# Context stream handled beside x in the first stage, own buffers for modulation blocks, and a later place for the last part of the filter network

## The chip, the core and the metric

The kernel runs on one core of a Trainium2 chip. The core has a matrix engine (PE, with its weight loads shown as PEld), a vector engine (DVE), an activation engine (ACT), a general engine (POOL, GpSimd) and a queue engine (SP) that issues most of the loads from memory. Each engine works through its own list of instructions in order and waits on semaphores for the others. The metric is device time in microseconds (us), the median of several runs; less is better.

## What is computed

Two layers of a diffusion backbone over 256 latent tokens with 2048 channels, with 256 context tokens beside them in the first layer. Cut to what matters here:

```python
sh1, sc1, g1, sh2, sc2, g2 = split(silu_c @ ada_w[l] + ada_b[l], 6)
h = rmsnorm(x, norm_g[l, 0]) * (1.0 + sc1) + sh1
# even layer (l = 0)
cmod = split(silu_cc @ ada_w[l][:, :2 * D_MODEL] + ada_b[l][:2 * D_MODEL], 2)
hc = rmsnorm(ctx, norm_g[l, 0]) * (1.0 + cmod[1]) + cmod[0]
y = hgrn_conv_mixer(h, hc, w_in, ...)       # first step: h @ w_in, and hc @ w_in[:, :3072]
x = x + g1 * y
x = x + g2 * (square(relu((rmsnorm(x) * (1 + sc2) + sh2) @ w1)) @ w2)
# odd layer (l = 1): Hyena. Its filters do not depend on x:
hdn = sin(freq * (z @ fw1 + fb1)); hdn = sin(freq * (hdn @ fw2 + fb2)); hdn = sin(freq * (hdn @ fw3 + fb3))
filt = hdn @ fw4
```

All products are made from fp32 values that are split into a high part and a low part, with three matmuls for each product (high by high, high by low, low by high).

## The kernel before

**The first stage** (`layer0` up to `pump_to(56)`) multiplies both streams, x and the context, with the first 3072 columns of the input weights ("w0"). The 2048 rows of the product (the channels) come in 16 tiles of 128, called kt. What a tile needs before its first matmul is its modulation: `ada_start(kt)` loads two blocks of 1 MB (shift and scale) and multiplies them on PE with both conditioning vectors (L212), ACT copies the result (L528), two small matmuls pick the rows (L531) and DVE adds the bias into `mod` (L533). `h_make` then makes the high and low parts of the normed tile, `hh` and `hl` for x, `uh` and `ul` for the context (L542 to L551). The norm's inverse root `rstd` of each stream is `norm_rstd` (L321 on PE, then L310 to L315).

The tiles are taken in four blocks of 1, 2, 5 and 8 (KBLOCKS). A block runs over column chunks: three of 1024 columns in block 0 and block 1, twelve of 256 in blocks 2 and 3. In each chunk the weights are loaded into a `raw` buffer (L660), ACT makes `whi` (L151), DVE makes `wlo` (L152), and PE multiplies the x side and then the context side (`block_mm`, L574 and L577). The results are added into `zz`, `v` for x and `czz`, `cv` for the context (L589 by ACT in block 0; L591, L595 by DVE later).

At the head of each chunk, `self.pump(1)` loads one further modulation block of 1 MB, which DVE multiplies by `sil` (L182; "PUMP" in the words below). While block b runs, `ada_start` is called for the tiles of block b + 1.

**Buffers.** All of these loads (w0 chunks, both blocks of `ada_start`, PUMP blocks) share the pool tag `raw`, with three buffers of 1 MB. A load is issued by SP, in SP's order, when the buffer's last reader is done.

**Order.** The statements inside `with self.in_order()` (block 0 and the preparation of tiles 0 to 2) keep the written order on each compute engine. Everywhere else a list scheduler, run when the program is built, fixes the order of each engine.

**The filter network.** `filter_net` runs on POOL from the start for more than 1300 us. Its last layer, `filter_tail`, transposes its result `h2` on PE (L1124, L1128), lets DVE scale it (`cv`, L1130), lets POOL take two sines of 29 instructions each (L1156 to L1181), and has DVE split the result into `h3h`, `h3l` (L1138, L1139). It stands in the loops of the first MLP, `mlp_body(0)`; the split is first used at the start of `hyena`. One step of those loops, `gemm_as`, makes 96 matmuls of 512 columns in eight half-megabyte pieces, each with one `whi` and one `wlo`.

Of the kernel before, what the change touches and what calls it, by code (L numbers as in the profile page):

```python
# [12 lines left out]
F32 = mybir.dt.float32  # L13
# [3 lines left out]
U8 = mybir.dt.uint8  # L17
# [4 lines left out]
P = 128  # L22
D = 2048
T = 256
KT = 16
# [38 lines left out]
class Kernel:  # L64
# [396 lines left out]
    def layer0(self):  # L461
# [3 lines left out]
        def s8(name, shape, dt=F32):  # L465
            t = pa.tile(shape, dt, tag="s8", name=name, bufs=3)
            return t

        silt = self.silt
        cct = pa.tile([P, 2, 2, KT], F32, tag="s2", name="cct", bufs=3)  # L470
        nc.sync.dma_start(out=cct[:, 0], in_=I["cct"])
# [9 lines left out]
        for lst, src in ((xq, "xT"), (cq, "ctxT")):  # L481
            for g in range(4):
                t = self.quad("x4", F32)
                nc.sync.dma_start(out=t[:, :, :T], in_=I[src][:, g * 4:g * 4 + 4, :])
                lst.append(t)
            if src == "xT":
                first = [self.ada_load(0, ch, 0, fa[:, ch, :]) for ch in range(2)]
                nc.sync.dma_start(out=self.sm, in_=I["sm"])
                chunks, _ = phase0_chunks()
                w0 = I["w0"]  # L490
                k0, nkt, row = chunks[0]
                assert nkt == 1
                loads = []
                for c0, cw, off in row:
                    r = fw[:, c0:c0 + cw]
                    nc.sync.dma_start(out=r, in_=bass.AP(w0.tensor, w0.offset + off, [[cw, P], [1, cw]]))
                    loads += [(c0, r[:, g * 256:g * 256 + 1024], list(range(g, g + 4)))
                              for g in range(0, cw // 256, 4)]
        ahead = {kt: [self.ada_load(0, ch, kt, s8("first", [P, D]) if kt == 2 and ch else None) for ch in range(2)]
                 for kt in kb[1]}  # L500
        xf = lambda kt: xq[kt // 4][:, kt % 4, :T]
        cf = lambda kt: cq[kt // 4][:, kt % 4, :T]
        nc.vector.memset(self.onesd, 1.0 / D)
        make_identity(nc, self.ident)
        masks = pa.tile([P, len(LEVELS), P], U8, name="masks")

# [15 lines left out]
        def ada_start(kt, raws=None):  # L522
            ps = self.psx()
            for ch in range(2):
                r = raws[ch] if raws else self.ada_load(0, ch, kt)
                self.ada_mm(ps[:, ch * P:(ch + 1) * P], r)
            sb = self.tmp(2 * P, "sq", 2)
            nc.scalar.activation(out=sb, in_=ps[:, :2 * P], func=AF.Copy)  # L528
            for ch in range(2):
                o = 2 * P + ch * 2  # L530
                nc.tensor.matmul(ps[:, o:o + 2], lhsT=sb[:, ch * P:(ch + 1) * P], rhs=self.selr, start=True,  # L531
                                 stop=True)
            self.last = nc.vector.tensor_tensor(  # L533
                out=view(self.mod, kt, [[192, 2], [16, 2]]), in0=view(ps, 2 * P, [[1, 2], [2, 2]]),
                in1=view(self.sm, SM["adab"][0] + kt, [[0, 2], [16, 2]]), op=ALU.add).ins
# [62 lines left out]
        with self.in_order():  # L598
# [10 lines left out]
            for i in range(4):  # L609
                square(xq, qx, i)  # L610
            for i in range(1, 4):
                qadd(nc.vector, qx, 0, i)
            rst.append(self.norm_rstd([qx[0][:, j, :T] for j in range(4)]))
            ada_start(0, first)
# [8 lines left out]
            for n, (c0, _, cgs) in enumerate(loads):  # L623
                block_mm(0, 0, 1, c0, *units[n], cgs, [0], 0, self.psx)
                if n < 2:
                    square(cq, qc, n * 2)
                    square(cq, qc, n * 2 + 1)
            ada_start(1, ahead[1])
            for i in range(1, 4):
                qadd(nc.vector, qc, 0, i)  # L630
            rst.append(self.norm_rstd([qc[0][:, j, :T] for j in range(4)]))
            h_make(0, 1, 1)
            for n, (c0, _, cgs) in enumerate(loads):
                block_mm(0, 0, 1, c0, *units[n], cgs, [0], 1)
            for side in range(2):
                h_make(1, 2, side)
            ada_start(2, ahead[2])
            for side in range(2):
                h_make(2, 3, side)
        self.filter_net(self.last)  # L640
# [4 lines left out]
        nc.vector.scalar_tensor_tensor(out=self.sil, in0=self.sil, scalar=1.0, in1=sr, op0=ALU.add, op1=ALU.mult)  # L645
        lbt = self.lb_setup()
        for b, (k0, nkt, row) in list(enumerate(chunks))[1:]:
# [35 lines left out]
        self.pump_to(56)  # L683
        self.ada_stop = 72
        self.new_u()
        self.dump("zz", zz)
# [25 lines left out]
        def s2(name):  # L712
            t = pa.tile([P, 512], F32, tag="s2", name=name, bufs=3)
            return t
# [33 lines left out]

        gh = pa.tile([P, NH], F32, name="gh")
        nc.vector.tensor_scalar(out=gh, in0=self.s_("gn", 0, 8), scalar1=0.5, scalar2=None, op0=ALU.mult)  # L750
        onehot = pa.tile([P, NH, NH], F32, name="onehot")
        nc.vector.memset(onehot, 0.0)
# [11 lines left out]
        def group(g0, par):  # L764
            qg = qq[g0 // 4][:, g0 % 4:g0 % 4 + G, :T]
            kq = s8("kq", [P, 4, W]) if par == 0 else st["kq1"]
            at = pa.tile([P, G, 2, T], F32, tag="s4", name="at", bufs=2)
            kd = s2("kd")
# [69 lines left out]
        def readout():  # L838
            rr = self.rsqrt(st["msq"][:NH, :T], NH, T)
            sel = pa.tile([NH, NH, P], F32, tag="s4", name="sel", bufs=2)  # L840
# [51 lines left out]
        for hh in range(2):  # L892
            nc.sync.dma_start(out=self.x[:, hh * 8:hh * 8 + 8, :], in_=I["xT"][:, hh * 8:hh * 8 + 8, :])
        self.pump_until(0, 2)

# [36 lines left out]

    def lb_setup(self):
        nc, cp = self.nc, self.cp
        self.zeros = self.pa.tile([P, T], F32, name="zeros")
        nc.vector.memset(self.zeros, 0.0)
        lg = self.s_("lb", 0, 48).rearrange("p (d l h) -> p d l h", d=2, l=3)
        mx = self.pa.tile([P, 2, NH], F32, name="lbm")
        e = self.pa.tile([P, 2, 3, NH], F32, name="lbe")
        s = cp.tile([P, 2, NH], F32, name="lbs")  # L940
# [37 lines left out]
    def mlp_body(self, l):  # L978
# [6 lines left out]
        for c in range(4):  # L985
# [10 lines left out]
            for g in range(4):  # L996
                if c == 3 and g == 2:
                    self.pump_to(self.ada_stop)
                if c == 2 and g == 0 and l == 0:
                    self.filter_tail()  # L1000
# [532 lines left out]
```

## Time and profile before

| what | us |
|---|---|
| median of 3 runs (2953.35 to 2958.92) | 2955.95 |
| the profiled execution | 2951.54 |
| its span, first to last instruction | 2949.7 |
| PE busy in it | 2788.0 (95%) |
| DVE busy | 2156.1 (73%) |
| POOL busy | 1560.0 (53%) |
| ACT busy | 1257.8 (43%) |

The profiled execution is one run, 4.4 us below the median; 1.8 us of it lie outside the span. An engine's busy time says little by itself: PE is the busiest, so what counts is the time in which PE stands, or runs at the lower of its two clocks (1.2 instead of 2.4 GHz). "PEclk" is the granted clock as a share of the higher one.

### The profile page before, as it was taken

The numbers are of one execution on the slowest core, as the hardware profiler recorded it, in microseconds if no ns is written. First come the engines' busy times: TensorE is split into PE (matmuls) and PEld (weight loads), VectorE is DVE, ScalarE is ACT, GpSimd is POOL, SyncE is SP. The second block draws the span as 40 slices with busy tenths as digits, with TensorE's granted clock in tenths as the row PEclk, the third lists the DMA queues.
The fourth block names the chain that finished last, engine by engine and source line by source line (L and its number), as shares of the span: only waits on it lengthen the run. The fifth ranks groups of instructions, "written<-read, shape, count | busy, mean of one in ns | idle before, by whom it ended". The sixth has DMA issues, their size and how long they took to land.

```text
span 2949.7 us, 46145 instructions
## 1 busy us (share of the span) xinstructions
PE 2788.0 (95%) x18508; PEld 2456.1 (83%) x18508; DVE 2156.1 (73%) x2599; ACT 1257.8 (43%) x1674; POOL 1560.0 (53%) x1716
## 2 busy tenths in 40 slices
PE   5887999999989999998999999999989999999997
PEld 4777999988987888887888989999988888888885
DVE  4766659998798878886778999998765555445455
ACT  4211224334445444343444545555455444353443
POOL 5999999999999999997000455455100000000000
PEclk8888999999999999999999999999999999999998
DMA  6776544445667787876877545444545555555552
GB/s 219 273 255 232 194 147 180 170 160 213 265 234 270 302 315 298 317 295 247 319 295 279 191 162 186 174 171 178 191 176 210 216 217 180 194 179 189 184 180 113
DMA packets 97862, 646.48 MB, mean 219 GB/s; under 512 B 11672, under 2 KB 15832, under 8 KB 22256
## 3 DMA queue, kind: packets, MB, share of 16 engines
q1 hardware_dynamic: 96464, 640.35, 58.1%
q0 software_dynamic: 1184, 3.18, 0.6%
q8 instruction: 145, 2.38, 0.3%
q14 instruction: 69, 0.57, 0.1%
HBM read 641.39 MB, written 2.10 MB: 218 GB/s over the span
## 4 chain that ended last, share of the span: by engine, by line
PE 61%; DVE 13%; DMA 2%; POOL 2%; issue 1%; ACT 1%; DVEq 0%; SPq 0%; ACTq 0%; POOLq 0%
PE acc L287 47%; PE acc L266 10%; DVE wlo L152 3%; PE aux L301 1%; DVE yl L158 1%; DMA raw<-in_w 1%; DVE p L928 1%; DVE cv L1295 1%; PE aux L1206 1%; DMA raw<-in_hy 1%; DVE y L1326 1%; DVE y L1329 1%; DVE y L1327 1%; DVE p L930 1%; ACT whi L151 0%
## 5 line engine op out<-in xcount | busy, mean ns | idle before, releaser
L152 DVE TENSOR_TENSOR wlo<-raw,whi 128x1024 fp32r<-128x1024 f32 (+1 forms) x778 | 1024.6, 1320 | 536.3 <-ACT whi L151 534.4
L151 ACT ACTIVATE whi<-raw 128x1024 fp32r<-128x1024 f32 (+1 forms) x806 | 843.8, 1049 | 1100.1 <-PE acc L287 718.0
L1027 POOL TENSOR_TENSOR xT<-xT,rstd 128x256 f32<-128x256 f32 x6 | 5.2, 898 | 849.8 <-DVE rstd L315 849.8
L287 PE MATMUL acc<-whi,hh 128*128 128x512 f32 x1024 | 403.2, 399 | 11.0 <-ACT hh L426 11.0
L266 PE MATMUL acc<-hh,whi 128*128 128x258 f32 (+1 forms) x1408 | 408.3, 290 | 0.0
L287 PE MATMUL acc<-whi,uh 128*128 128x512 f32 x1024 | 405.6, 396 | 0.0
L287 PE MATMUL acc<-whi,hl 128*128 128x512 f32 x1024 | 402.1, 398 | 3.6 <-DVE hl L427 3.6
L287 PE MATMUL acc<-whi,ul 128*128 128x512 f32 x1024 | 405.0, 396 | 0.0
L266 PE MATMUL acc<-hh,wlo 128*128 128x258 f32 (+1 forms) x1408 | 400.1, 284 | 3.8 <-DVE wlo L152 3.7
L266 PE MATMUL acc<-hl,whi 128*128 128x258 f32 (+1 forms) x1408 | 399.1, 284 | 0.0
L287 PE MATMUL acc<-wlo,uh 128*128 128x512 f32 x1024 | 282.3, 396 | 8.9 <-DVE wlo L152 8.9
L287 PE MATMUL acc<-wlo,hh 128*128 128x512 f32 x1024 | 279.5, 395 | 0.0
L266 PEld LDWEIGHTS acc<-hh,whi 128*128 128x128 f32 x1408 | 267.1, 190 | 7.7 <-issue 7.1
L266 PEld LDWEIGHTS acc<-hh,wlo 128*128 128x128 f32 x1408 | 266.7, 189 | 6.6 <-DVE wlo L152 4.6
L266 PEld LDWEIGHTS acc<-hl,whi 128*128 128x128 f32 x1408 | 268.2, 190 | 0.6 <-issue 0.4
L287 PEld LDWEIGHTS acc<-whi,hh 128*128 128x128 f32 x1024 | 193.5, 189 | 56.5 <-ACT hh L426 12.1
L287 PEld LDWEIGHTS acc<-wlo,uh 128*128 128x128 f32 x1024 | 193.2, 189 | 54.2 <-DVE wlo L152 9.3
L182 DVE SCALAR_TENSOR_TENSOR araw<-araw,sil 128x2048 f32<-128x2048 f32 x96 | 235.6, 2455 | 0.0
L287 PEld LDWEIGHTS acc<-whi,hl 128*128 128x128 f32 x1024 | 193.3, 189 | 47.9 <-DVE hl L427 5.2
L287 PEld LDWEIGHTS acc<-whi,uh 128*128 128x128 f32 x1024 | 193.0, 188 | 45.4 <-issue 0.3
L287 PEld LDWEIGHTS acc<-wlo,hh 128*128 128x128 f32 x1024 | 193.0, 188 | 45.3
L287 PEld LDWEIGHTS acc<-whi,ul 128*128 128x128 f32 x1024 | 192.9, 188 | 44.7
(361 smaller groups left out, 5788.0 us busy)
## 6 DMA issues: line engine op xcount, KB each, us to landing
raw<-in_m SPq DMA_DIRECT2D x256, 1024.0 KB, 4.8
araw<-in_ada SPq DMA_DIRECT2D x96, 1024.0 KB, 5.4
raw<-in_ada SPq DMA_DIRECT2D x93, 1024.0 KB, 4.9
raw<-in_w SPq DMA_DIRECT2D x71, 1024.0 KB, 4.9
raw<-in_hy SPq DMA_DIRECT2D x48, 1024.0 KB, 4.8
raw<-in_ho SPq DMA_DIRECT2D x16, 1024.0 KB, 4.9
raw<-in_w SPq DMA_DIRECT2D x12, 640.0 KB, 6.6
fr<-in_fw SPq DMA_DIRECT2D x16, 256.0 KB, 5.1
```

What stands on the lines that cost most here:

```text
L151: nc.scalar.activation(out=hi[:, :w], in_=src, func=AF.Copy)
L152: e.tensor_tensor(out=lo[:, :w], in0=src, in1=hi[:, :w].bitcast(F32), op=ALU.subtract)
L158: return (eng or nc.vector).tensor_tensor(out=lo, in0=src, in1=hi.bitcast(F32), op=ALU.subtract)
L182: self.hold(nc.vector.scalar_tensor_tensor(out=r, in0=r, scalar=0.5, in1=self.sil, op0=ALU.mult, op1=ALU.mult, accum_out=self.mod[:, idx:i ...
L266: m = nc.tensor.matmul(acc[:, :n], lhsT=w[:, s], rhs=x(kt, n), start=hn == 0 and j == 0 and pn == 0, stop=hn == 1 and j == 7 and pn == 2).ins
L287: nc.tensor.matmul(acc[th], lhsT=x(kt)[:, th * P:(th + 1) * P], rhs=w[:, j * 512:(j + 1) * 512], start=kt == 0 and w is hi and x is xhi, s ...
L301: nc.tensor.transpose(out=tp[:, j * T + th * P:j * T + th * P + P], in_=src[th][:, f * P:(f + 1) * P], identity=self.ident)
L928: nc.vector.scalar_tensor_tensor(out=c3[:, :, 1:], in0=u3[:, :, :63], scalar=w0, in1=c3[:, :, 1:], op0=ALU.mult, op1=ALU.add)
L930: nc.vector.scalar_tensor_tensor(out=c3[:, :, :63], in0=u3[:, :, 1:], scalar=w2, in1=c3[:, :, :63], op0=ALU.mult, op1=ALU.add)
L1206: nc.tensor.matmul(o, lhsT=cf[wi][:, a, i * P:(i + 1) * P], rhs=src[xi][:, a, :], start=pn == 0, stop=pn == 2)
L1295: nc.vector.tensor_scalar(out=t, in0=t, scalar1=acc[:, T:T + 1], scalar2=None, op0=ALU.add)
L1326: nc.vector.tensor_tensor(out=t1, in0=zr, in1=ha, op=ALU.mult)
```

## The change

- The context tiles are loaded right behind the x tiles, ahead of the first modulation blocks and weights. Their squares are taken on ACT right behind those of x; their three additions go from DVE to POOL (`qadd(nc.gpsimd, qc, ...)`). The context's `norm_rstd` and its first `h_make` are written between the second and the third part of the x side of block 0, and the preparation of tiles 1 and 2 is spread between the parts of the context side.
- A new pool `p0` holds two buffers `rawx` of 1 MB for the blocks of `ada_start`. The `raw` ring of three now serves w0 chunks and PUMP blocks (and one block of tile 2). `p0` is closed behind the first stage, and a new pool `pz` (`zeros`, `masks` and work tiles of the recurrence, which were in `pa`) takes its place; its fills therefore come at the end of the stage instead of at the start.
- `filter_tail` moves from the third quarter of the MLP's loop (c = 2, g = 0 of the second product) to the fourth (c = 3, g = 1).
- The inverse root is the same in both kernels.

```diff
+        s0, s1 = ExitStack(), ExitStack()
+        p0 = s0.enter_context(tc.tile_pool(name="p0", bufs=1))
+
+        def rawx():
+            t = p0.tile([P, D], F32, tag="rawx", name="rawx", bufs=2)
+            return t
...
-        ahead = {kt: [self.ada_load(0, ch, kt, s8("first", [P, D]) if kt == 2 and ch else None) for ch in range(2)]
-                 for kt in kb[1]}
+        ahead = {1: [self.ada_load(0, ch, 1, rawx()) for ch in range(2)],
+                 2: [self.ada_load(0, ch, 2, None if ch else s8("first", [P, D])) for ch in range(2)]}
...
-                r = raws[ch] if raws else self.ada_load(0, ch, kt)
+                r = raws[ch] if raws else self.ada_load(0, ch, kt, rawx())
...
             for i in range(4):
                 square(xq, qx, i)
+            for i in range(4):
+                square(cq, qc, i)
             for i in range(1, 4):
                 qadd(nc.vector, qx, 0, i)
+                qadd(nc.gpsimd, qc, 0, i)
...
             for n, (c0, _, cgs) in enumerate(loads):
                 block_mm(0, 0, 1, c0, *units[n], cgs, [0], 0, self.psx)
-                if n < 2:
-                    square(cq, qc, n * 2)
-                    square(cq, qc, n * 2 + 1)
+                if n == 1:
+                    rst.append(self.norm_rstd([qc[0][:, j, :T] for j in range(4)]))
+                    h_make(0, 1, 1)
             ada_start(1, ahead[1])
-            for i in range(1, 4):
-                qadd(nc.vector, qc, 0, i)
-            rst.append(self.norm_rstd([qc[0][:, j, :T] for j in range(4)]))
-            h_make(0, 1, 1)
             for n, (c0, _, cgs) in enumerate(loads):
                 block_mm(0, 0, 1, c0, *units[n], cgs, [0], 1)
-            for side in range(2):
-                h_make(1, 2, side)
-            ada_start(2, ahead[2])
-            for side in range(2):
-                h_make(2, 3, side)
+                if n == 0:
+                    for side in range(2):
+                        h_make(1, 2, side)
+                    ada_start(2, ahead[2])
+                if n == 1:
+                    for side in range(2):
+                        h_make(2, 3, side)
...
+        s0.close()
+        pz = s1.enter_context(tc.tile_pool(name="pz", bufs=1))
...
-                if c == 2 and g == 0 and l == 0:
+                if c == 3 and g == 1 and l == 0:
                     self.filter_tail()
```

**PE between the two sides of block 0.** The names: `hh`, `hl` are x, `uh`, `ul` the context, `sq_...` with `onesd` is `norm_rstd`, `silt` a tile's modulation, `selr` its two small matmuls. Before:

```order
L577 MATMUL aux<-wlo,hh 128x256
L212 MATMUL aux<-raw,silt 32x128 x32
L531 MATMUL aux<-selr,sq 128x2 x2
L321 MATMUL aux<-sq_256,onesd 128x256 x4
L574 MATMUL acc<-uh,whi 128x256
```

And now:

```order
L578 MATMUL aux<-hh,wlo 128x256
L321 MATMUL aux<-sq_153,onesd 128x256 x4
L581 MATMUL aux<-whi,hh 128x256
...
L212 MATMUL aux<-rawx,silt 32x128 x32
L535 MATMUL aux<-selr,sq 128x2 x2
L578 MATMUL acc<-uh,whi 128x256
...
L212 MATMUL aux<-first,silt 32x128 x16
L212 MATMUL aux<-raw,silt 32x128 x16
L535 MATMUL aux<-selr,sq 128x2 x2
L578 MATMUL acc<-uh,whi 128x256
```

The context's norm has moved ahead of the last 24 matmuls of the x side, and the modulation of tile 2 into the context side (after 24 of its 72 matmuls).

**SP from the first modulation block ahead to the second w0 chunk of block 1** (`in_w` is w0, `in_ada` modulation, `in_c` the conditioning vector). Before:

```order
L163 DMA raw<-in_ada 128x2048 x3
L163 DMA first<-in_ada 128x2048
...
L643 DMA raw<-in_c 128x2048
L163 DMA raw<-in_ada 128x2048
L660 DMA raw<-in_w 128x2048
L163 DMA raw<-in_ada 128x2048 x5
L660 DMA raw<-in_w 128x2048
```

And now:

```order
L163 DMA rawx<-in_ada 128x2048 x2
L163 DMA first<-in_ada 128x2048
L163 DMA raw<-in_ada 128x2048
...
L648 DMA raw<-in_c 128x2048
L163 DMA raw<-in_ada 128x2048
L163 DMA rawx<-in_ada 128x2048 x2
L665 DMA raw<-in_w 128x2048
L163 DMA rawx<-in_ada 128x2048
L163 DMA raw<-in_ada 128x2048
L163 DMA rawx<-in_ada 128x2048
L665 DMA raw<-in_w 128x2048
```

Between two w0 chunks there is now one `raw` load, and the others have their own two buffers; the order of the queue is otherwise alike.

**DVE between the scaling and the split of the filter's last layer.** Before (in full):

```order
L1130 TENSOR_SCALAR cv_13728<-aux,f3v 128x256
L152 TENSOR_TENSOR wlo<-raw,whi 128x1024
L182 SCALAR_TENSOR_TENSOR araw,mod<-araw,sil 128x2048
L152 TENSOR_TENSOR wlo<-raw,whi 128x1024 x2
...
L1008 TENSOR_TENSOR y<-acc,y 128x512 x2
L152 TENSOR_TENSOR wlo<-raw,whi 128x1024 x4
...
L1138 CAST h3h<-cv_13730 128x256
L1139 TENSOR_TENSOR h3l<-cv_13730,h3h 128x256
```

And now:

```order
L1139 TENSOR_SCALAR cv_15208<-aux,f3v 128x256
...
L930 SCALAR_TENSOR_TENSOR xT<-aux,mod,xT 128x256 x4
L402 SCALAR_TENSOR_TENSOR hl<-xT,gv,hh 128x256
L414 TENSOR_TENSOR ssum<-ssum,sq 128x256
...
L182 SCALAR_TENSOR_TENSOR araw,mod<-araw,sil 128x2048 x2
L152 TENSOR_TENSOR wlo<-raw,whi 128x1024 x3
L182 SCALAR_TENSOR_TENSOR araw,mod<-araw,sil 128x2048 x2
L1147 CAST h3h<-cv_15210 128x256
```

In both, 11 `wlo` of 1024 columns, 4 products by `sil` and 2 additions into `y` stand between the two; now 4 residuals `xT`, 4 `hl` and 5 additions into `ssum` stand there too.

## Rows read from the trace of the kernel before

**Rows 1.** Windows by stage: us, busy PE, PEld, DVE, ACT, POOL, clock, DMA, GB/s

```profile
0.00:26.00 26.00, 7.26 (x78) 5.29 (x78) 12.51 (x45) 11.37 (x15) 3.92 (x12) 1.00 0.93 324
26.00:36.60 10.60, 10.33 (x70) 9.93 (x70) 2.22 (x2) 8.16 (x13) 0.00 (x0) 0.84 0.99 398
36.60:55.40 18.80, 6.33 (x77) 4.75 (x77) 9.67 (x12) 3.41 (x8) 15.50 (x25) 0.67 0.34 121
55.40:78.70 23.30, 15.66 (x149) 14.55 (x149) 10.29 (x15) 13.84 (x20) 22.79 (x39) 0.79 0.21 65
78.70:139.50 60.80, 54.49 (x631) 50.25 (x632) 44.13 (x67) 11.44 (x20) 59.47 (x90) 0.90 0.76 286
139.50:295.00 155.50, 126.33 (x1264) 118.49 (x1262) 99.02 (x158) 29.07 (x50) 152.05 (x219) 0.86 0.70 247
295.00:400.00 105.00, 104.64 (x878) 104.64 (x879) 67.96 (x88) 28.56 (x27) 102.15 (x140) 1.00 0.52 190
```

**Rows 2.** Timeline of PE: start, length, instruction, idle time before it and releaser

```profile
18.66 2.18 PE L212 MATMUL aux<-fa,silt 128*32 128x128 f32 x64
...
44.86 3.75 PE L321 MATMUL aux<-sq,onesd 128*128 128x256 f32 x8 [4.50 <-DVE sq L512]
55.38 0.58 PE L574 MATMUL acc<-uh,whi 128*128 128x256 f32 x1 [6.77 <-ACT uh L550]
```

**Rows 3.** Loads of the first 36 us: GB/s in 40 slices; KB each, median us to landing

```profile
GB/s 0 4 57 308 277 89 199 240 338 379 373 366 402 445 437 419 414 446 376 430 414 414 388 372 369 346 349 363 391 395 422 428 437 428 410 428 428 437 394 298
...
fa<-in_ada SPq DMA_DIRECT2D x2, 1024.0 KB, 11.2
```

**Rows 4.** Timeline of SP: start, length and issue of the first modulation blocks

```profile
3.84 2.33 SPq L163 DMA_DIRECT2D fa<-in_ada  x2
```

**Rows 5.** Timeline of ACT: evictions of the x side's last part

```profile
36.62 2.09 ACT L589 ACTIVATE v<-aux 128x512 f32<-128x512 f32 x4
```

**Rows 6.** Who waited for whom on SP, 60 to 295 us: total, times, longest

```profile
SPq L163 <- PE aux L212: 37.2, 17, 6.2
SPq L660 <- PE aux L212: 34.4, 4, 28.0
```

**Rows 7.** Who waited for whom on PE, 78 to 295 us

```profile
PE aux L212 <- DMA raw<-in_ada: 11.6, 8, 3.6
PE acc L574 <- ACT whi L151: 8.2, 3, 3.9
PE acc L577 <- DVE wlo L152: 6.4, 2, 3.3
PE acc L574 <- DVE wlo L152: 5.5, 4, 3.0
```

**Rows 8.** Loads from 70 to 310 us: KB each, median us to landing

```profile
raw<-in_ada SPq DMA_DIRECT2D x44, 1024.0 KB, 6.0
```

**Rows 9.** DVE from 139.5 to 295 us by group: busy, mean ns, idle before

```profile
L182 DVE SCALAR_TENSOR_TENSOR raw<-raw,sil 128x2048 f32<-128x2048 f32 x13 | 32.5, 2497 | 0.0
...
L595 DVE TENSOR_TENSOR zz<-acc,zz 128x256 f32<-128x256 f32 x16 | 6.4, 418 | 24.9 <-PE acc L574 24.9
```

**Rows 10.** The page, part 5: the low parts made by DVE, whole run

```profile
L152 DVE TENSOR_TENSOR wlo<-raw,whi 128x1024 fp32r<-128x1024 f32 (+1 forms) x778 | 1024.6, 1320 | 536.3 <-ACT whi L151 534.4
```

**Rows 11.** Who waited for whom around the filter's tail, 1341 to 1400 us

```profile
DVE h3h L1138 <- POOL cv L1181: 14.3, 1, 14.3
...
POOL sfp L1156 <- DVE cv L1130: 9.7, 1, 9.7
...
PE acc L287 <- DVE wlo L152: 8.9, 1, 8.9
```

**Rows 12.** Windows around the filter's tail; columns as in rows 1

```profile
1350.66:1381.50 30.84, 30.84 (x134) 24.93 (x133) 24.66 (x21) 11.68 (x11) 29.36 (x28) 1.00 0.77 299
1381.50:1395.90 14.40, 8.63 (x38) 6.63 (x36) 0.06 (x2) 3.19 (x3) 12.79 (x29) 0.96 0.26 99
...
1399.10:1410.00 10.90, 10.90 (x36) 8.68 (x37) 10.14 (x10) 3.15 (x3) 0.00 (x0) 0.73 0.80 293
```

More of the change, by code (lines that the diff above doesn't have):

```diff
@@ L467, in s8 @@
             return t
+        s0, s1 = ExitStack(), ExitStack()
[3 more added lines that the diff above has]
+            return t
         silt = self.silt
-        cct = pa.tile([P, 2, 2, KT], F32, tag="s2", name="cct", bufs=3)
+        cct = p0.tile([P, 2, 2, KT], F32, name="cct")
         nc.sync.dma_start(out=cct[:, 0], in_=I["cct"])
@@ L485, in layer0 @@
                 lst.append(t)
[L486 to L498, printed above, removed]
-        ahead = {kt: [self.ada_load(0, ch, kt, s8("first", [P, D]) if kt == 2 and ch else None) for ch in range(2)]
-                 for kt in kb[1]}
+        first = [self.ada_load(0, ch, 0, fa[:, ch, :]) for ch in range(2)]
+        nc.sync.dma_start(out=self.sm, in_=I["sm"])
+        chunks, _ = phase0_chunks()
+        w0 = I["w0"]
+        k0, nkt, row = chunks[0]
+        assert nkt == 1
+        loads = []
+        for c0, cw, off in row:
+            r = fw[:, c0:c0 + cw]
+            nc.sync.dma_start(out=r, in_=bass.AP(w0.tensor, w0.offset + off, [[cw, P], [1, cw]]))
+            loads += [(c0, r[:, g * 256:g * 256 + 1024], list(range(g, g + 4))) for g in range(0, cw // 256, 4)]
+        ahead = {1: [self.ada_load(0, ch, 1, rawx()) for ch in range(2)],
+                 2: [self.ada_load(0, ch, 2, None if ch else s8("first", [P, D])) for ch in range(2)]}
         xf = lambda kt: xq[kt // 4][:, kt % 4, :T]
@@ L504, in layer0 @@
         make_identity(nc, self.ident)
-        masks = pa.tile([P, len(LEVELS), P], U8, name="masks")
         def square(src, q, g):
@@ L645, in layer0 @@
         nc.vector.scalar_tensor_tensor(out=self.sil, in0=self.sil, scalar=1.0, in1=sr, op0=ALU.add, op1=ALU.mult)
-        lbt = self.lb_setup()
+        lbt = self.lb_setup(p0)
         for b, (k0, nkt, row) in list(enumerate(chunks))[1:]:
@@ L684, in layer0 @@
         self.ada_stop = 72
+        s0.close()
+        pz = s1.enter_context(tc.tile_pool(name="pz", bufs=1))
+        masks = pz.tile([P, len(LEVELS), P], U8, name="masks")
+        self.zeros = pz.tile([P, T], F32, name="zeros")
+        nc.vector.memset(self.zeros, 0.0)
         self.new_u()
@@ L712, in s2 @@
         def s2(name):
-            t = pa.tile([P, 512], F32, tag="s2", name=name, bufs=3)
+            t = pz.tile([P, 512], F32, tag="s2", name=name, bufs=3)
             return t
@@ L747, in ctx_states @@
             self.dump("S", S)
-        gh = pa.tile([P, NH], F32, name="gh")
+        gh = pz.tile([P, NH], F32, name="gh")
         nc.vector.tensor_scalar(out=gh, in0=self.s_("gn", 0, 8), scalar1=0.5, scalar2=None, op0=ALU.mult)
-        onehot = pa.tile([P, NH, NH], F32, name="onehot")
+        onehot = pz.tile([P, NH, NH], F32, name="onehot")
         nc.vector.memset(onehot, 0.0)
@@ L766, in group @@
             kq = s8("kq", [P, 4, W]) if par == 0 else st["kq1"]
-            at = pa.tile([P, G, 2, T], F32, tag="s4", name="at", bufs=2)
+            at = pz.tile([P, G, 2, T], F32, tag="s4", name="at", bufs=2)
             kd = s2("kd")
@@ L839, in readout @@
             rr = self.rsqrt(st["msq"][:NH, :T], NH, T)
-            sel = pa.tile([NH, NH, P], F32, tag="s4", name="sel", bufs=2)
+            sel = pz.tile([NH, NH, P], F32, tag="s4", name="sel", bufs=2)
             nc.sync.dma_start(out=sel, in_=I["sel"])
@@ L893, in layer0 @@
             nc.sync.dma_start(out=self.x[:, hh * 8:hh * 8 + 8, :], in_=I["xT"][:, hh * 8:hh * 8 + 8, :])
+        s1.close()
         self.pump_until(0, 2)
@@ L931, in conv, with lb_setup @@
                                        op0=ALU.mult, op1=ALU.add)
-    def lb_setup(self):
+    def lb_setup(self, p0):
         nc, cp = self.nc, self.cp
-        self.zeros = self.pa.tile([P, T], F32, name="zeros")
-        nc.vector.memset(self.zeros, 0.0)
         lg = self.s_("lb", 0, 48).rearrange("p (d l h) -> p d l h", d=2, l=3)
-        mx = self.pa.tile([P, 2, NH], F32, name="lbm")
-        e = self.pa.tile([P, 2, 3, NH], F32, name="lbe")
+        mx = p0.tile([P, 2, NH], F32, name="lbm")
+        e = p0.tile([P, 2, 3, NH], F32, name="lbe")
         s = cp.tile([P, 2, NH], F32, name="lbs")
```

## The prediction

> **What bounds the kernel now.** The whole-run busy share of PE is 95%, so I first looked for the 5%, with the windows by stage: the reader is to see in [rows 1] that in the first 295 us PE is busy for only 7.3 + 10.3 + 6.3 + 15.7 + 54.5 + 126.3 = 220 us, that its clock there is 0.67 to 0.90 of the higher one in four of the rows, and that from 295 us on it is full at clock 1.00. The loads do not fill the time either: the DMA share is above 0.9 only until 36.6 us, falls to 0.34 and 0.21, and is 0.70 to 0.76 afterwards. So the first stage is a chain of waits, and this is where three of the four edits lie.
>
> Stage A, to 55.4 us, ends with the first matmul of the context side. PE is idle 4.5 us before the context's norm, works on it for 3.75 us at the lower clock, and is idle 6.8 us behind it [rows 2]. Stage B, to 78.7 us, is the context side of block 0 and the wait for block 1's first weights. The queue view says why they are late: the longest wait of a w0 load on SP is 28.0 us, until PE has multiplied a modulation block [rows 6]; all three `raw` buffers hold modulation ahead. Stages C (block 1, to 139.5 us) and D (block 2, to 295 us) wait in turns for modulation loads (11.6 us), for high parts, that is for w0 loads (8.2), and for low parts (6.4 + 5.5) [rows 7].
>
> The second place is the filter's tail: DVE waits 14.3 us for POOL's second sine, and PE runs dry for 8.9 us behind it [rows 11], then works 10.9 us at clock 0.73, which costs another 10.9 × 0.27 = 2.9 us [rows 12]. The present tail costs about 12 us.
>
> **The change part by part.** Full-rate prices first: 878 instructions in 104.64 us give 0.119 us a matmul [rows 1], and a modulation block pair 2.18 us for its 64 [rows 2].
>
> *Start of x.* Four context loads of 512 KB (2.1 MB) now run ahead of the first modulation pair. At the 410 GB/s or so of that time [rows 3] this is 5.1 us. The pair was issued at 3.84 [rows 4] and landed 11.2 us later [rows 3], at 15.0 and about 1.5 us later; PE took it at 18.66 behind the x norm [rows 2]. So about 2 us of the delay are hidden, and x's matmuls start 3.3 us later. The weights come behind it in the queue and slip by the same 5.1 us, which the longer modulation path just covers. POOL's three additions are covered: it is busy for 3.9 us of the first 26 and not at all to 36.6 [rows 1], and their result is wanted at 36.
>
> *Order of the two sides.* The x side of block 0 took 10.6 us from 26.0 for its 72 matmuls [rows 1], so its first 48 took 7.1; now they end at 29.3 + 7.1 = 36.4. The context's norm follows at once (2.2 us, between 3.75 at the lower clock and half of it), to 38.6. The chain behind it to the first `uh` was 6.8 us [rows 2]; PE covers 2.8 us of it with the last 24 x matmuls, then stands, since `v` is evicted on ACT behind `uh` and a PSUM bank for the next modulation comes free with the first of these four evictions (2.09 / 4 = 0.52 us each [rows 5]). `uh` at 45.4, the modulation multiplied to 48.1, its copy and selection 1.0 us: the context side starts at 49, not 55.4. **A: 6.4 us gained.** The two additional activation-table loads lie beside DVE's reciprocals.
>
> *Stage B.* The context side is 72 matmuls, 8.6 us, with some 2 us more while the clock recovers, plus the modulation of tile 2 in its midst (2.2) and the wait for its copy and selection (some 2): 15 us. The first w0 load of block 1 now waits only for that modulation, about 54 us; with the 6.0 us of a load [rows 8] and two conversions it is ready at 62, inside the 15 us. I take 15.5 in place of 23.3: **7.8 gained.** If the load were late as now, nothing is gained here.
>
> *Stage C.* Its 631 instructions are 288 matmuls, 320 modulation multiplies (five tiles) and selections: 34.3 + 10.9 + 2 = 47 us at full rate against 60.8. The second w0 load still needs the first PUMP done, and that waits for `sil`, behind the first addition of the block; I leave 6 us for this and for the clock: 53. **7.8 gained**, between 0 and 13.8.
>
> *Stage D.* 720 matmuls, 512 modulation multiplies and eight selections: 85.7 + 17.4 + 4 = 107 us at full rate, 8.9 a chunk, against 155.5. It cannot reach 107: in the DVE order of some chunks the low part stands behind the previous chunk's last addition and its PUMP, so that after PE's last matmul come 2 × 0.42 + 2.50 [rows 9] + 1.32 [rows 10] = 4.7 us before PE can go on with its remaining 52 matmuls (6.2): 10.8 us a chunk. Seven chunks of twelve are such before, five now: 120 us before, 116 now. Before, the other 35 us are late loads and the low clock that follows. With PUMP and w0 alone in the ring of three, a w0 load is released one chunk ahead, some 9 us for a 6.0 us load; but SP still holds it behind `rawx` loads that wait for PE (37.2 us of such waits now [rows 6]). I leave 16 of the 35: 132. **23.5 gained**, between 0 (155.5) and 39 (116).
>
> *End of the stage.* The fills that moved there are some ten short DVE instructions: 1 us lost.
>
> *The tail's place.* POOL had waited 9.7 us for PE's scaled input [rows 11], and the sine began at 1350.7 [rows 12], so its network ends at about 1341; with PE 45 us earlier, the old place would have made PE wait for POOL for most of that, and the gain would have been lost. In the new place, some 200 us of PE work later, POOL is long done. What the tail costs there: 11 low parts of half a piece each still stand between scaling and split, 31 us of PE work, and the same two sines follow. POOL's first took the 30.8 us in which DVE was busy for 24.7; the second took 14.4 with DVE standing [rows 12]. DVE now has 13 short instructions more in these 31 us (0.42 each by the additions [rows 9], some 5.5 us), so it is nearly full, and reaches the split when the first sine is about done, as now. I take the same 12 us: **nothing gained or lost**; the h3 parts are still ready before their use.
>
> By the Trainium skill (SBUF — State Buffer, section "SBUF: two separate sides") DVE instructions with two SBUF inputs and GpSimd hold a shared port pair for a whole instruction and the other blocks. The trace agrees: 28 POOL instructions took 29.4 us beside a busy DVE, 29 took 12.8 beside an idle one [rows 12]. By the rows the sum stays at 2911; by the rule taken strictly, a DVE list without gaps leaves POOL no turn at all, and it would be 2925.
>
> **Sum.** 6.4 + 7.8 + 7.8 + 23.5 − 1 = 44.5 us. The span of 2949.7 becomes 2905.2, the profiled execution 2907; the median lies 4.4 us above its execution, so 2911.5.
>
> **The rivals.**
> - *Half the gain.* SP's order binds, not the buffers: a w0 load behind a `rawx` that waits for PE is as late as before. Then C and D give some 8 together: 6.4 + 7.8 + 8 − 1 = 21, 2935. For it: the SP waits on PE's modulation are the largest group [rows 6]. Against: the two kinds no longer take each other's buffers.
> - *No late load is left.* D falls to 116 and C to 50: 6.4 + 7.8 + 11 + 39 − 1 = 63, 2893. Against it: 247 GB/s must become 330 in D, which only the start shows [rows 1].
> - *The tail grows.* If POOL gets no turn beside the fuller DVE list, both sines follow at DVE's standstill: a wait of 2 × 14 = 28 us instead of 14.3, 14 us more: 2925. Against it: it got 28 instructions done beside 21 of DVE [rows 12], and there are now some 34.
> - *The pair of `rawx` buffers is the new neck (slower).* A tile's loads now need the previous tile's multiplies; before, any of three buffers could take them. If each of the 13 later tiles left PE waiting for the release and a full 6.0 us load [rows 8], with half as much again for the slow clock behind it, 13 × 9 = 117 us would be lost where 11.6 of wait, some 18 with the clock, are lost now [rows 7]. It decides from some 5 us a tile (18 + 44.5 = 62 over 13 tiles); at 6 a tile the result is 2970. Against it: consecutive multiplies of a tile stand 45 to 120 matmul rows apart on PE, 5 to 14 us, so only the closest pairs can wait, and for 1 to 3 us.
> - *No change.* The order and the start of x take back what the buffers give: 2955.
>
> **How the numbers follow.** Chances: the forecast 0.55 (2895 to 2925 by the bounds of C and D), half the gain 0.16, no late load 0.09, the tail grows 0.10, no change 0.04, the new neck 0.06. The predicted time is that of the first, 2911. A range from 2886 to 2942 holds the first, the second, the third and the fourth, 0.9 with its edges cut. A change of 0.2% (5.9 us) is about what this measurement can tell: faster 0.90, the same 0.04, slower 0.06.
>
> **What would show it.** In the changed profile: x's first full-rate matmuls 3 us later; the context side's first matmul near 49 us; no wait of some 28 us of a w0 load on SP; PE in block 2 at clock above 0.9 for some 130 us, and the full-rate stretch starting near 250 us, not 295; a DVE wait of 12 to 16 us at `h3h` about 140 us later than now, with 8 to 10 us of PE idle behind it. The prediction is wrong if PE waits on `rawx` loads for more than 25 us in all, if the idle time of block 2 stays at 29 us, or if the wait at `h3h` is over 25 or gone.

## The result, and the profile after

| kernel | median, us | runs | range | ratio to before, 95% interval |
|---|---|---|---|---|
| before | 2957.43 | 4 | 2953.35 to 2959.39 | |
| changed | 2902.63 | 4 | 2901.76 to 2904.56 | 0.9817 [0.9800, 0.9834] |

The change takes 54.8 us off the median; 2911 was forecast. The two profiled executions, 2951.54 and 2903.24, differ by 48.3, and the traces are compared on these.

The windows of the changed kernel by stage (columns as in [rows 1]; its cuts and these lie near each other, not on the same matmuls: 40.6 is ahead of the end of the x side at 42.8, and 124.5 and 241.7 are ahead of the next block's first matmul, where 139.5 and 295.0 are behind it):

```profile
0.00:30.30 30.30, 9.11 (x78) 6.41 (x78) 14.71 (x34) 16.97 (x20) 11.07 (x15) 0.86 0.95 334
30.30:40.60 10.30, 10.27 (x61) 10.05 (x62) 2.77 (x4) 6.28 (x10) 2.34 (x6) 0.75 0.97 382
40.60:51.60 11.00, 6.78 (x89) 5.90 (x87) 5.26 (x7) 3.25 (x7) 10.22 (x19) 0.73 0.36 129
51.60:71.70 20.10, 16.91 (x208) 16.18 (x209) 9.90 (x15) 10.31 (x19) 19.58 (x37) 0.81 0.40 140
71.70:124.50 52.80, 48.79 (x564) 45.07 (x562) 44.49 (x66) 14.25 (x22) 51.73 (x71) 0.97 0.87 336
124.50:241.70 117.20, 110.41 (x1266) 105.30 (x1265) 96.96 (x168) 27.07 (x48) 115.04 (x147) 0.99 0.79 294
```

So the stages are measured from first matmul to first matmul. PE's timeline, block 2's and block 3's first matmul, in the kernel before and then in the changed one:

```profile
138.28 0.28 PE L574 MATMUL acc<-hh,whi 128*128 128x256 f32 x1
293.38 0.28 PE L574 MATMUL acc<-hh,whi 128*128 128x256 f32 x1
```

```profile
125.66 0.38 PE L578 MATMUL acc<-hh,whi 128*128 128x256 f32 x1
244.56 0.39 PE L578 MATMUL acc<-hh,whi 128*128 128x256 f32 x1 [2.65 <-ACT whi L151]
```

Stages B and C (from the context side's first matmul to block 2's; one more tile is now multiplied in B, so they are compared together) take 74.1 us instead of 82.9. Block 2 takes 118.9 instead of 155.1, and the clock in it is 0.99 instead of 0.86 [rows 1]. Block 3 begins 48.8 us earlier. In front of all this little is won: the context side starts at 51.6 instead of 55.4, and the clock there is still 0.73 to 0.81.

PE's timeline in that front (the first of x's unbroken matmuls, the context's norm, the modulation multiplies of tile 1, and the selection of tile 2's rows):

```profile
30.33 0.58 PE L578 MATMUL aux<-hh,wlo 128*128 128x256 f32 x1 [0.55 <-DVE wlo L628]
38.11 1.89 PE L321 MATMUL aux<-sq,onesd 128*128 128x256 f32 x8
46.56 3.64 PE L212 MATMUL aux<-rawx,silt 128*32 128x128 f32 x64 [3.72 <-ACT v L593]
61.63 0.61 PE L535 MATMUL aux<-selr,sq 128*128 128x2 f32 x4 [3.19 <-ACT sq L532]
```

The context's norm no longer waits and takes 1.89 us, not 3.75 [rows 2]. But the 64 modulation multiplies of tile 1 take 3.64 us here, and took 1.95 in the kernel before.

Who waited for whom on PE, 60 to 300 us (the groups over 0.5 us):

```profile
PE acc L578 <- DVE wlo L152: 4.4, 4, 2.0
PE acc L581 <- DVE wlo L152: 4.3, 4, 2.5
PE acc L578 <- ACT whi L151: 3.9, 4, 2.6
PE aux L535 <- ACT sq L532: 3.8, 2, 3.2
```

The line on modulation loads (11.6 us in [rows 7]) is gone. SP's modulation loads, 60 to 260 us, still wait for PE, longer than the 37.2 us in [rows 6]:

```profile
SPq L163 <- PE aux L212: 55.9, 17, 11.7
```

The w0 loads no longer wait for PE in this stretch; in [rows 6] these waits were 34.4 us, one of them 28.0.

The tail in its new place, who waited for whom between 1480 and 1640 us:

```profile
PE aux L301 <- DVE y L1017: 8.8, 1, 8.8
...
DVE h3h L1147 <- POOL cv L1190: 9.8, 1, 9.8
```

and the windows there:

```profile
1545.00:1556.00 11.00, 2.22 (x10) 1.42 (x8) 1.36 (x3) 0.89 (x1) 8.72 (x21) 0.77 0.29 119
1556.00:1566.00 10.00, 10.00 (x38) 8.10 (x37) 10.00 (x16) 5.43 (x10) 0.00 (x0) 0.74 0.43 152
```

It is the same hole as in [rows 11, 12]: 8.8 us of PE idle and 10 us at 0.74, some 11 us.

### The profile page after: what moved, and what is told of

The parts are those of the page before. It is cut to its first block, busy times and chain, and to the rows that moved or that the text cites. A ratio compares the mean times of both kernels' runs of the same rounds, so it can differ in the third digit from the quotient of the medians.

```text
span 2901.5 us, 46145 instructions
## 1 busy us (share of the span) xinstructions
PE 2773.3 (96%) x18508; PEld 2445.9 (84%) x18508; DVE 2163.2 (75%) x2596; ACT 1261.4 (43%) x1676; POOL 1629.4 (56%) x1719
## 4 chain that ended last, share of the span: by engine, by line
PE 64%; DVE 12%; POOL 2%; issue 1%; ACT 1%; DMA 1%; DVEq 0%; SPq 0%; ACTq 0%; POOLq 0%
PE acc L287 47%; PE acc L266 12%; DVE wlo L152 2%; PE aux L301 1%; DVE yl L158 1%; PE aux L1215 1%; DVE p L939 1%; DVE cv L1304 1%; DVE y L1338 1%; PE aux L1350 1%; DVE p L941 1%; DVE y L1336 1%; DVE y L1335 1%; PE aux L212 1%; DVE Z L1276 0%
## 5 line engine op out<-in xcount | busy, mean ns | idle before, releaser
L182 DVE SCALAR_TENSOR_TENSOR araw<-araw,sil 128x2048 f32<-128x2048 f32 x96 | 242.4, 2526 | 0.0
L287 PEld LDWEIGHTS acc<-wlo,hh 128*128 128x128 f32 x1024 | 193.0, 189 | 45.6
```

What stands on the lines that cost most here:

```text
L182: self.hold(nc.vector.scalar_tensor_tensor(out=r, in0=r, scalar=0.5, in1=self.sil, op0=ALU.mult, op1=ALU.mult, accum_out=self.mod[:, idx:i ...
L287: nc.tensor.matmul(acc[th], lhsT=x(kt)[:, th * P:(th + 1) * P], rhs=w[:, j * 512:(j + 1) * 512], start=kt == 0 and w is hi and x is xhi, s ...
```

## The experiments

Theory: the own buffers give the gain in blocks 1 and 2; the later tail gives little itself, but without it PE waits for POOL's network and the gain is lost; the rearranged front gives a few us. Rivals: the front carries it; or the tail's place has nothing to do with it. All times are medians; "changed" is 2902.6.

| run | median, us | ratio to before, 95% |
|---|---|---|
| old_tail | 2955.31 | 0.9994 [0.9984, 1.0003] |
| shared_ring | 2936.52 | 0.9923 [0.9902, 0.9945] |
| own_buffers | 2906.37 | 0.9832 [0.9817, 0.9847] |
| late_tail_only | 2948.61 | 0.9970 [0.9958, 0.9982] |
| pool_split | 2901.43 | 0.9814 [0.9799, 0.9830] |
| early_tail | 2898.68 | 0.9807 [0.9793, 0.9822] |
| early_tail_pool | 2891.62 | 0.9782 [0.9768, 0.9797] |
| weights_first | 2910.59 | 0.9845 [0.9831, 0.9860] |
| adds_on_dve | 2892.85 | 0.9795 [0.9780, 0.9810] |
| front_dve | 2887.35 | 0.9776 [0.9760, 0.9791] |

The last two ran on a chip on which the kernel before took 2951.74; beside the other runs it took 2957.2 to 2958.0.

**old_tail**

```diff
-                if c == 3 and g == 1 and l == 0:
+                if c == 2 and g == 0 and l == 0:
                     self.filter_tail()
```

> The changed kernel with one line put back: the filter's tail stands at its old place (third part of the MLP, first group) again. In the changed kernel's trace POOL's network ended only at 1402.2 us, and PE would reach the tail's transposes about 50 us earlier than before, near 1290. Theory (the later place banks the gain): PE stands until POOL is done; some 10 us after PE stops, DVE is dry too and POOL runs its remaining instructions at the rate it has beside an idle DVE (12.8 us for 29 against 29.4 for 28), so the 110 us left shrink to about 50: 2903 + 40 to 55 = 2943 to 2958, with one PE wait of that size on a POOL result at the transpose line. Rival (the place is worth nothing by itself, since POOL's work is done in time): no such wait, the same 10 us of idle time at the split, 2903 within 5.

The whole gain is gone. PE's longest wait of the run:

```profile
PE aux L1133 <- POOL fxn L1190: 61.2, 1, 61.2
```

PE stands for 61.2 us at the tail's transposes until POOL's network is done. The theory holds; the wait is a little longer than expected, since the front was quicker in this execution (below).

**shared_ring**

```diff
-                r = raws[ch] if raws else self.ada_load(0, ch, kt, rawx())
+                r = raws[ch] if raws else self.ada_load(0, ch, kt)
```

> The changed kernel, but the modulation loads of the later blocks go into the ring of three shared with the w0 loads again (one call put back); order of the front, loads ahead and the tail's place stay. Theory (own buffers give blocks 1 and 2 their gain): block 2 takes some 150 us again instead of 117 and block 1 some 58 instead of 53, with PE waits on modulation loads and on high parts back: 2903 + 30 to 46 = 2933 to 2949. Rival (the rearranged front gives it, since block 1's first weights were late for its order): block 2 stays under 125 us and the time within 8 us of 2903.

33.9 us lost, with the front as changed. Its blocks 1 and 2 in windows, then PE's waits from 60 to 300 us:

```profile
68.50:134.40 65.90, 55.37 (x630) 50.27 (x629) 48.76 (x71) 16.97 (x27) 64.49 (x95) 0.87 0.73 269
134.40:280.40 146.00, 123.61 (x1268) 115.86 (x1267) 97.50 (x156) 28.97 (x50) 142.95 (x200) 0.88 0.72 262
```

```profile
PE aux L212 <- DMA raw<-in_ada: 11.5, 7, 3.6
PE acc L578 <- ACT whi L151: 7.6, 4, 2.7
```

Modulation loads are late for 11.5 us again, as in [rows 7], and the clock is back at 0.87 and 0.88. From the context side's first matmul at 51.0 us to block 3's at 280.3 it takes 229.3 us, in the changed kernel 193.0, so the buffers are worth 36.3 us there, of which 33.9 reach the end.

**own_buffers** (load order and order of block 0 as in the kernel before; buffers and tail as changed)

```diff
-        ahead = {1: [self.ada_load(0, ch, 1, rawx()) for ch in range(2)],
-                 2: [self.ada_load(0, ch, 2, None if ch else s8("first", [P, D])) for ch in range(2)]}
+        ahead = {kt: [self.ada_load(0, ch, kt, s8("first", [P, D]) if kt == 2 and ch else None) for ch in range(2)]
+                 for kt in kb[1]}
...
-            for i in range(4):
-                square(cq, qc, i)
...
-                qadd(nc.gpsimd, qc, 0, i)
```

> The opposite half: own buffers for the later blocks' modulation loads and the new place of the tail, but the front (order of loads, of the two norms and of block 0's parts, loads ahead) as in the kernel before. Theory: block 2 takes 117 to 120 us as in the changed kernel; what is lost is the 14 us by which the changed kernel ends block 1 earlier, in part: 2903 + 6 to 15 = 2909 to 2918. Rival (the front carries the gain): block 2 takes 140 us or more, and the time is 2930 or more.

Only 3.7 us lost. Blocks 1 and 2:

```profile
74.90:126.40 51.50, 49.68 (x561) 45.51 (x561) 48.45 (x75) 12.64 (x21) 50.59 (x68) 0.95 0.84 320
126.40:244.00 117.60, 108.92 (x1266) 103.71 (x1265) 96.70 (x168) 28.19 (x50) 115.36 (x144) 1.00 0.82 305
```

Block 2 is as short as in the changed kernel, and B and C together take 70.3 us (56.1 to 126.4). So the buffers and the tail's place carry 51 of the 55 us, and the front's rearrangement 3.7, less than the theory's 6 to 15. Where these 3.7 arise stays open: the two profiles are level at block 3's first matmul (244.0 here, 244.6 in the changed kernel).

Not run: one ring of five buffers for all these loads. The two `rawx` are also two buffers more, and no run tells whether the gain needs buffers of their own or only more of them.

**late_tail_only** (the kernel before with the tail at c = 3, g = 1)

> The kernel before with only the tail's place moved to the later one of the changed kernel. There POOL's network ended at 1340.9 and POOL then waited 9.7 us for PE, so the tail was not waited for by PE at its old place. Theory (the move gives nothing by itself, it only lets the gain of the buffers pass): DVE waits 8 to 16 us for the second sine near 1600 instead of 1395, 2957 within 4. Rival (the later place itself shortens the tail): 2945 to 2950.

Neither fits: 8.6 us faster, though its profiled execution shows the same hole as the changed kernel (DVE 9.8, PE 8.8 us). What differs is the spread: ten runs from 2938.09 to 2953.16, where 13 of the kernel before lie between 2952.87 and 2959.05, and ten of old_tail between 2952.20 and 2957.81. My reading: at the old place PE and POOL are about level, so an execution whose front goes better only waits longer for POOL, and the time is pinned; the later place lets it through. No run shows this by itself, but the traces bear it out. In the kernel before PE reaches the tail's first transpose at 1342.4, only 1.5 us behind the end of POOL's network; the 9.7 us of the expectation also hold all that lies between this transpose and DVE's scaling. In late_tail_only's profile PE passes the old place 4.5 us earlier (its transposes of `r` there begin at 1337.8 instead of 1342.2), and POOL's network ends at 1346.6. With the tail at the old place PE would have stood for some 9 us, by an estimate from these times.

**pool_split, early_tail, early_tail_pool: what the remaining hole needs**

```diff
-        nc.vector.tensor_copy(self.h3h, h3)
-        nc.vector.tensor_tensor(out=self.h3l, in0=h3, in1=self.h3h.bitcast(F32), op=ALU.subtract)
+        nc.gpsimd.tensor_copy(self.h3h, h3)
+        nc.gpsimd.tensor_tensor(out=self.h3l, in0=h3, in1=self.h3h.bitcast(F32), op=ALU.subtract)
```

> The changed kernel with the split of the filter's result into high and low part (two instructions) on POOL, right behind POOL's second sine, instead of on DVE. Theory (DVE's wait for the second sine is what the tail costs): DVE's 9.8 us of waiting and PE's 8.8 us of idle time behind it go, and the 10 us at clock 0.74 behind them (2.6 us): 2903 - 9 to 12 = 2891 to 2894. The second sine then takes 25 to 35 us beside a busy DVE and ends near 1562, before the first use near 1588. Rival (POOL and DVE share a port, so DVE pays for the sine in longer instructions where it paid by standing): the DVE instructions of those 30 us grow, PE still runs dry for 5 us or more, 2898 to 2903.

1.2 us won, within the scatter. The hole moved on: windows, the waits of DVE and PE, and POOL's end of the second sine in pool_split:

```profile
1530.00:1562.00 32.00, 32.00 (x145) 26.07 (x144) 32.00 (x36) 14.26 (x19) 30.52 (x28) 1.00 0.61 241
```

```profile
PE aux L301 <- DVE y L1017: 5.7, 1, 5.7
DVE ss L1238 <- ACT ss L1237: 5.5, 1, 5.5
```

```profile
1562.58 1.33 POOL L1190 TENSOR_TENSOR cv<-sfq,sfp 128x128 f32<-128x128 f32 x1
```

Beside a DVE without a gap (32.00 of 32 us) the second sine takes 33.0 us and ends at 1563.9. POOL's next work, the sums for the first filter taps, is then late for ACT and DVE, and PE runs dry for 5.7 us behind them. So the rival's numbers came true (5 us or more, 2898 to 2903), but its cause only in part: beside the sine DVE's instructions do grow (11 `wlo` of 1.36 us each, against 1.24 in early_tail_pool from 1500 to 1580 us, where POOL mostly stands), by some 3 us in the 32, while the wait ahead of PE's gap is that of the next reader of POOL. So the tail needs more lead as well:

```diff
+                if c == 3 and g == 2 and l == 0:
+                    self.filter_tail()
                 rate = RATES["m1", l] if c or g else 0
...
-                if c == 3 and g == 1 and l == 0:
-                    self.filter_tail()
```

> The same earlier place of the tail, but the split stays on DVE. In DVE's order it stands 18 instructions behind the scaling, as before and after (18 to 19). Theory (the distance in DVE's order between scaling and split sets the wait, not the place in the program): DVE again waits 8 to 16 us for the second sine, PE runs dry for some 9 us behind it, 2902 within 4. Rival (the place is what matters): the wait is under 4 us, 2890 to 2895.

> The changed kernel with the filter's tail two m1 groups and three m2 groups earlier (fourth part of the MLP, third m1 group, which PE reaches near 1430 us) and the split on POOL behind the second sine. In the changed kernel POOL's network ended at 1402.2, so PE should not wait for it. Theory (in the run with the split on POOL alone the wait only moved on, to the first filter window's scaling, for which POOL was 5.5 us late; with 70 us more of lead nobody waits): both sines run beside a busy DVE, 22 to 32 us each, and end near 1500; no PE idle time of 5 us or more between 1400 and 1600; 2902 - 9 to 12 = 2890 to 2893. Rival (POOL's work always costs DVE and so PE the same time, wherever it stands): 2899 or more.

In early_tail, with the split on DVE, the wait is there again (who waited for whom, 1400 to 1620 us), and 3.9 us are won, at the edge of what was expected:

```profile
PE acc L287 <- DVE wlo L152: 5.1, 1, 5.1
...
DVE h3h L1147 <- POOL cv L1190: 11.0, 1, 11.0
```

In early_tail_pool PE waits nowhere for more than 1.9 us from 1400 to 1620. POOL's timeline (start and end of the sines, the split's high part, first tap):

```profile
1438.41 0.30 POOL L1165 TENSOR_SCALAR sfp<-cv 128x128 f32<-128x128 f32 x1 [41.83 <-DVE cv L1139]
...
1493.62 0.46 POOL L1190 TENSOR_TENSOR cv<-sfq,sfp 128x128 f32<-128x128 f32 x1
1494.14 0.40 POOL L1147 CAST h3h<-cv 128x256 fp32r<-128x256 f32 x1
1558.11 0.73 POOL L1235 TENSOR_TENSOR sw<-fr 128x256 f32<-128x256 f32 x1 [62.75 <-DVE ssum L414]
```

11.0 us won, the size of the hole. Engine and place are both needed: one alone gave 1.2, the other 3.9.

**weights_first** (the context's loads behind block 0's weights again, the rest as changed)

```diff
+        load4(xq, "xT")
         first = [self.ada_load(0, ch, 0, fa[:, ch, :]) for ch in range(2)]
...
+        load4(cq, "ctxT")
         ahead = {1: [self.ada_load(0, ch, 1, rawx()) for ch in range(2)],
```

> The changed kernel with the four context loads behind the first modulation pair and block 0's weights again, as in the kernel before; the rest as changed. Theory (the 2.1 MB ahead of the modulation pair delayed x's first full-rate matmul by 4.3 us): x's first matmul some 4 us earlier (24 to 25 instead of 28.7), the context loads land by 31 us all the same, and block 1 begins 2 to 4 us earlier: 2898 to 2901. Rival (the chain behind the context's norm sets the end of block 0, or the low clock takes the lead back): 2902 within 1.5.

8.0 us slower, against both. PE's timeline, and ACT's, ahead of x's first matmul:

```profile
30.65 1.01 PE L538 MATMUL aux<-selr,sq 128*128 128x2 f32 x4 [10.28 <-ACT sq L535]
```

```profile
23.07 1.06 ACT L516 ACTIVATE sq<-x 128x1024 f32<-128x1024 f32 x1 [4.16 <-DMA x<-in_ctxT]
...
29.91 0.42 ACT L312 ACTIVATE rstd<-rs_q 128x256 f32<-128x256 f32 x1
30.24 0.37 ACT L535 ACTIVATE sq<-aux 128x256 f32<-128x256 f32 x1
```

In ACT's fixed order the context's squares stand ahead of x's inverse root and of the copy of the modulation. With the context loaded late they block both: x starts at 35.1 instead of 28.7. I had left this out: the load order is tied to the order of the squares. The next two runs start from early_tail_pool and untie it.

**adds_on_dve and front_dve**

```diff
             for i in range(1, 4):
                 qadd(nc.vector, qx, 0, i)
-                qadd(nc.gpsimd, qc, 0, i)
...
+            for i in range(1, 4):
+                qadd(nc.vector, qc, 0, i)
             for n, (c0, _, cgs) in enumerate(loads):
                 block_mm(0, 0, 1, c0, *units[n], cgs, [0], 0, self.psx)
```

and for front_dve also the load order of weights_first, with the context's squares moved to the same place, ahead of its additions.

> The kernel with the early tail and the split on POOL (2891.6), and the three additions of the context's squares on DVE, behind block 0's low parts, instead of on POOL. Theory (POOL's additions slowed DVE's x norm: its fifth instruction took 2.46 us beside them and 0.42 beside an idle POOL): that instruction takes 0.4 us again, x's first matmul comes 1 to 2 us earlier (27 to 28 us), and the context's norm no later: 2889 to 2891. Rival (x then waits for block 0's weights, which land at 26.5, and the low clock evens it out): the instruction shrinks but the time stays 2891.6 within 1.5.

> As the run beside it, with the context's loads behind block 0's weights as in the kernel before, and the context's squares behind block 0's conversions on ACT, so that nothing of the context stands ahead of x on any engine. In the run with the loads alone put back, ACT's copy of the modulation waited 10.28 us behind the context's squares. Theory (the order of ACT and the order of the loads have to go together): x's first matmul near 24 us, the context's norm near 33 instead of 38, the context side's first matmul at 44 to 47 instead of 51, and 2885 to 2889. Rival (the low clock that follows the shorter start takes it back, or PE waits for banks that ACT evicts late): 2890 to 2893.

The instruction of x's norm in question (L314, the fourth on DVE, which the expectation calls the fifth) in the changed kernel, and in adds_on_dve:

```profile
21.88 2.46 DVE L314 SCALAR_TENSOR_TENSOR rs_q<-rs_q,rs_v 128x256 f32<-128x256 f32 x1
```

```profile
22.28 0.42 DVE L314 SCALAR_TENSOR_TENSOR rs_q<-rs_q,rs_v 128x256 f32<-128x256 f32 x1
```

POOL's additions did cost DVE 2.0 us on x's chain, but x's first matmul came at 28.9 all the same, since PE then waited for the first modulation blocks. The rival holds: no gain (by the ratio to before, which allows for the other chip, 0.9795 against 0.9782). front_dve is 5.5 us faster than adds_on_dve on the same chip. Its PE timeline:

```profile
24.29 0.58 PE L581 MATMUL aux<-hh,whi 128*128 128x256 f32 x1 [1.58 <-ACT hh L557]
...
33.81 1.89 PE L321 MATMUL aux<-sq,onesd 128*128 128x256 f32 x8
42.17 3.21 PE L212 MATMUL aux<-rawx,silt 128*32 128x128 f32 x64 [3.64 <-ACT v L596]
```

x starts at 24.3, the norm at 33.8, the context side at 46.4, as expected. With the tail its median is the lowest here, 64.4 us under the kernel before on its chip, where the change won 54.8 on its own. That it beats early_tail_pool is not shown: that one is 65.6 us under the kernel before on another chip, and each of the two ratios lies within the other's interval.

## Why the prediction was right

The time was forecast 9 us too high (2911.5 against 2902.6). Some 5 of the 9 come from the step from the profiled execution to the median: I added 4.4 us, as in the kernel before, and here the median is 0.6 us below its execution. The stages themselves gave 48.2 us instead of 44.5. That this is so close is partly luck: A, B and C gave 9.4 us less than forecast, and D 12.7 more. By its steps, measured from first matmul to first matmul:

- **A, 6.4 us forecast, 3.8 measured; B and C, 7.8 + 7.8 against 8.8.** The chain of A was right, the clock was not. The profile of old_tail, whose program is the same up to the tail, happened to have a higher granted clock there:

```profile
28.70:48.30 19.60, 15.17 (x148) 13.96 (x149) 8.90 (x12) 11.20 (x18) 8.40 (x17) 1.00 0.76 283
48.30:63.00 14.70, 13.16 (x207) 12.42 (x206) 8.35 (x14) 8.82 (x16) 14.18 (x26) 1.00 0.57 215
63.00:118.00 55.00, 50.25 (x568) 46.29 (x564) 45.82 (x68) 15.90 (x25) 53.93 (x74) 0.94 0.86 323
```

  There the context side starts at 48.3, beside my 49, and B and C take 70.9 us (block 2's first matmul is at 119.2), where the forecast comes to 67.3. In the changed kernel's profile, at 0.73 to 0.81, the two are 51.6 and 74.1. So 6.5 us between the two profiles go with the clock; I had allowed some 2 us for it in B, and in C 6 us for it and for the wait for `sil` together. The other 3.6 us of B and C stay open.
- **Start of x: 3.3 us forecast, 4.3 measured.** The loads were put right. "Covered" was wrong for POOL's additions, at no price here, since the modulation came later still.
- **D, 23.5 forecast, 36.2 measured: the mis-sized term.** Of 35 us of late loads and low clock I kept 16, because SP would still hold w0 loads behind `rawx` loads that wait for PE. SP's modulation loads do wait for PE longer, 55.9 us, but PE waits for none of them, and for high parts only 3.3 us from 124.5 to 245 us, 2.65 of them at block 3's first matmul. My reading, which no run separates: a load that SP issues late is not late for PE when a whole chunk lies between. Of the 11.9 us left over the 107 at full rate, 6.1 are PE's waits for low parts, for which I had put 9. shared_ring and own_buffers show that this is the buffers' doing and not the front's.
- **End of the stage, 1 us lost: about right.** The lead of 48.8 us at block 3's first matmul is 49.3 at PE's last wait for the MLP's norm (849.31 instead of 898.65) and 48.2 at the end.
- **The tail: nothing gained or lost at the new place, the gain lost at the old.** Right, and here the case was decided: 52.7 us by old_tail. The wait at `h3h`, 9.8 us, is under the 12 to 16 that I gave, with the 8 to 10 of PE behind it. But that POOL's network would still end at 1341 was wrong. It ended 61 us later:

```profile
1400.83 1.32 POOL L1190 TENSOR_TENSOR fxn<-sfq,sfp 128x128 f32<-128x128 f32 x1
```

  In the 240 us from 60 to 300 POOL, busy nearly all the time, did 35 instructions fewer (fifth bracket; before, then changed), while DVE was busy for 185.5 us instead of 154.9:

```profile
60.00:300.00 240.00, 196.75 (x2061) 183.87 (x2061) 154.92 (x242) 54.22 (x89) 234.66 (x345) 0.87 0.68 243
```

```profile
60.00:300.00 240.00, 224.78 (x2406) 215.22 (x2407) 185.54 (x292) 65.65 (x99) 235.23 (x310) 0.98 0.73 272
```

  Where PE no longer waits, DVE is denser, and POOL's instructions get longer. By 1300 us the network is 49 instructions behind (1413 done instead of 1462); at the 1.19 us each that POOL then takes (86 in 102.2 us) these are 58 of the 61 us. The new place, at 1497, had 95 us to spare, so the error cost nothing; a place at 1350, safe by my number, would have made PE wait.
- **The rivals.** Half the gain and the new neck fell with PE's waits. No late load was near for D (118.9 us, where it had 116) and wrong for A, B and C. The tail did not grow: the first sine took 22.5 us, not longer than before (30.8 [rows 12]). By the Trainium skill (SBUF — State Buffer, section "SBUF: two separate sides") a DVE and a GpSimd instruction on the shared port pair exclude each other. The 2.46 and 0.42 us above, and the second sine's 33.0 us in pool_split against 14.4 at DVE's standstill [rows 12], agree that each waits for the other; that a DVE list without gaps leaves POOL no turn, as I had drawn from it, does not hold: 28 instructions got through beside 32.00 of 32 us.

## What to carry to other kernels

When two kinds of loads share a ring, count what PE's waits for them do to its clock too: here 11.6 us of waits for one kind and 8.2 for the other stood beside a clock of 0.86 to 0.90, and two more buffers, kept for one kind, gave 34 us. Before you bank a gain on one engine, look for a long background chain on another that has to be done at a fixed point of the program; it does not get faster, and may get slower, and its reader has to move by the gain and more. In a sum of stages, cut both traces at the same matmul: windows that are off by a wait put the gain into the wrong stage. When a wait at one reader is removed, look for the next reader of the same late engine, and give the chain lead as well as another consumer.

## What was not expected of the hardware

The same program up to the tail reached block 3 (its first matmul, behind a wait of some 2.5 us for a high part) at 244.6 us in the changed kernel's profile, at 237.8 in pool_split's and at 235.0 in old_tail's. Between the first and the last the difference begins in x's matmuls, which start 0.21 us apart until 35.2 us in the changed kernel and until 33.3 in old_tail, and 0.12 apart from there on; at their end it is 0.8 us. It grows at the first modulation multiplies behind the context's norm: 64 of them took 3.64 us or 1.95, with waits of 3.72 and 3.33 us ahead of them. Of the 6.8 us of pool_split little reaches the end, though its tail differs too: its span is 2900.8 and the changed kernel's 2901.5. What decides the level in such an execution stays open.
